# Delta rule layer: the fillers of a stage recorded ahead of the next query and merge, and the transposes of key and value heads 4 to 7 in the scans' Y banks

## The chip, the cores and the metric

One core of a Trainium2 chip runs the whole layer in one launch. The metric is the device time of one execution in microseconds; smaller is better. The engines are TensorE (PE; its weight loads are PEld), VectorE (DVE), ScalarE (ACT), GpSimd (POOL), and SyncE (SP), whose queue issues all DMAs here.

## The reference, cut to what matters

One layer on 1024 tokens of width 1024, with a context of 256 tokens: a token mixer (a Fourier branch and a gated delta rule in both directions, eight heads of 128), merged by gates, then a convolutional FFN. All in fp32. The change lies in the delta rule. For each head, the sequence is first projected and convolved to q, k and v; then per chunk of tokens a triangular system is solved and a state is carried from chunk to chunk:

```
l_mat = where(lower_strict, beta * (k k^T) * decay, 0)
u, w  = triangular_solve(l_mat, [v*beta, k*beta*exp(g)])     # unit diagonal
for each chunk:                                              # the scan
    v_new = u - w @ s
    o     = q_head @ s + (q k^T * decay) @ v_new
    s     = s * exp(g_last) + k_tail^T @ v_new
```

The scan of the context runs first, from a zero state, and gives the states from which the scans of the 1024 tokens start.

## The kernel before, in words

**How it is scheduled.** The program first records all operations, engine by engine and without running them (`Program.record`, L349 is the place where they are all issued later). Then it orders them itself (`schedule`): each operation has a cost in a table, and a rank, which is the longest path of costs behind it to the end of the program, plus a bonus, minus `MIX` = 0.1 of the TensorE cost of all that was recorded before it. Each engine gets its queue in the order in which this planner would start the operations; of those that are ready, the one of the highest rank goes first. The queues are then fixed, and each engine works its queue in order.

**Why the order of recording matters.** A tile is asked for by a tag, and the buffers of a tag are handed out in turn, in the order of recording. The next user of a buffer waits until all uses of the one before it are done. So two things recorded in one order keep it in every buffer that they share, whatever their ranks. PSUM has eight banks, one buffer each: `pp` and `pf` (projections; `pf` for the fillers later), `pd` (score products, query norms), `pm` (the merge), and `X0`, `X1`, `Y0`, `Y1` for the scans of direction 0 and 1. A bank is one buffer, also where only a part of it is used.

**The stages.** `ORDER` names ten stages: c0 and c1 are the context's scans for heads 0 to 3 and 4 to 7; x0 to x7 are the heads on the 1024 tokens, in the order c0, x0, x1, c1, x2 and on to x7. A stage needs, in this order: the projected query and the loaded key (`project_kq`; context stages project nothing there), the decay and score products (`ready_up`, bank `pd`), the inversion of 32x32 blocks on VectorE (`invert`, with a way out to DRAM and back on either side), the merge of those blocks to 128x128 ones by 32- and 64-wide products on TensorE (`merge`, bank `pm`), the loaded keys and values as tokens by channels (`load_kv`), and the scan (`scan_ctx`, `scan_head`). A scan's step of one direction is a chain through TensorE, VectorE and ScalarE: two products in X, then two in Y; with the output there are three. After the last step of a head's scan its outputs are transposed in Y0 and Y1 for a norm (`squares`), and the norm's row, transposed in Y1, is copied out.

**The fillers.** `sides(n)` records the next n projections of a list: k of heads 4 to 7, v of heads 4 to 7, z of eight heads, then gates. Pass 0 of the loop (scan c0) records k4 to k7, pass 1 (scan x0) v4 to v7, each later pass two of the others. `SIDES` has these numbers. A key or value projection (`project_kv`) has 24 matmuls of 256 columns for the context and 48 of 512 columns for the tokens, in three accumulations of which two fit the two banks; its result is convolved into a staging tile `xs`, of which there are two; then ten 128x128 transposes in three groups (`tt`) turn it, ScalarE copies each group out to a tile `tk` (two buffers), and a DMA stores it in DRAM, from where the scans load it. Of keys, ScalarE also squares the group in place. The weights of key, value and query projections go through one ring of three buffers for halves (tags `h`, `l`, each projection takes two of each). The z and gate fillers have weight buffers of their own, which come free when v7 is done.

Of the kernel before, what the change touches and what calls it, by code (L numbers as in the profile page):

```python
# [32 lines left out]
SIDES = (4, 4, 2, 2, 2, 2, 2, 2, 2, 2)  # L33
# [155 lines left out]
class Program:  # L189
# [14 lines left out]
    def close(self, p):  # L204
        self.events.append((False, p))
# [276 lines left out]
def body(tc, a, out):  # L482
    prog = Program(tc)
    layer(prog, a, out)
    prog.run()


def layer(prog, a, out):
# [14 lines left out]
    def ps(tag, shape, name):  # L503
        return psum.tile(shape, F32, tag=tag, name=name, bufs=PPB if tag == "pp" else 1)
# [3 lines left out]
    def bank(shape, name):  # L508
        rota[1] += 1
        return ps(rota[0][rota[1] % len(rota[0])], shape, name)  # L510
# [28 lines left out]
    def weights(src, name, eng=None, tags=("h", "l"), pl=None):  # L539
        return [halves(src[:, o:o + HALF], pl or wst, tags, f"{name}{o}", eng) for o in range(0, src.shape[-1], HALF)]  # L540

    def product(pt, wl, rhs, nk=KT):
        n = 0
        for k in range(nk):
            h, l = rhs(k)
            wh, wlo = wl[k // 4]
            ks = slice((k % 4) * P, (k % 4 + 1) * P)
            for w_, r_ in ((wh, h), (wh, l), (wlo, h)):
                te.matmul(pt, w_[:, ks], r_, start=n == 0, stop=n == 3 * nk - 1)
                n += 1  # L550
# [54 lines left out]
    XY = ("X0", "X1", "Y0", "Y1")  # L605
# [142 lines left out]
    def conv_taps(pt, acc, w3):  # L748
        n = acc.shape[-1]
        se.activation(acc, pt[:, 0:n], AF.Identity, scale=w3[:, 1:2])  # L750
        ve.scalar_tensor_tensor(acc[:, 1:n], pt[:, 0:n - 1], w3[:, 0:1], acc[:, 1:n], op0=ALU.mult, op1=ALU.add)
        ve.scalar_tensor_tensor(acc[:, 0:n - 1], pt[:, 1:n], w3[:, 2:3], acc[:, 0:n - 1], op0=ALU.mult, op1=ALU.add)

    def silu_of_half(acc, name):
        n = acc.shape[-1]
        for o in range(0, n, HALF):
            part = acc[:, o:min(o + HALF, n)]
            th_ = dt("th", f"{name}_{o}", part.shape)
            se.activation(th_, part, AF.Tanh)
            ve.scalar_tensor_tensor(part, th_, 1.0, part, op0=ALU.add, op1=ALU.mult)  # L760
# [79 lines left out]
    def invert_blocks(name, dl):  # L840
        dtt = dram.tile([2 * NU, P, 32], F32, tag="dt", name=f"dt_{name}", bufs=2)
        bl = dt("GR", f"BL_{name}", (P, 32, 32))
        bt = dt("CL", f"BT_{name}", (P, 16, 32))
        btf = bt.rearrange("n c i -> n (c i)")
        po.memset(btf, 0.0)
        for e in range(2):
            es = slice(e * NI, (e + 1) * NI)
            sp.dma_start(bl[es].rearrange("n i j -> n (i j)"), dl.rearrange("u (k i) j -> (u k) (i j)", k=4))
            po.memset(btf[es, e:HALF:34], 1.0)
        lt_ = bl.rearrange("n i j -> n j i")  # L850
        for j in range(31):
            r, w = 31 - j, j // 2 + 1
            tm = dt("tmp", f"tm_{name}{j}", (P, 144))[:, 0:r * w].rearrange("n (w r) -> n w r", r=r)
            ve.tensor_tensor(tm, bt[:, 0:w, j:j + 1].broadcast_to([P, w, r]),
                             lt_[:, j:j + 1, j + 1:32].broadcast_to([P, w, r]), op=ALU.mult)
            ve.tensor_tensor(bt[:, 0:w, j + 1:32], bt[:, 0:w, j + 1:32], tm, op=ALU.subtract)
        for e in range(2):
            sp.dma_start(dtt.rearrange("u (k c e) i -> e (u k) c i", k=4, e=2)[e], bt[e * NI:(e + 1) * NI])
        k2 = dt("CL", f"K2_{name}", (P, 2 * NU, 32))
        sp.dma_start(k2, dtt.rearrange("u p i -> p u i"))  # L860
        return k2
# [80 lines left out]
    def project_kv(w, h):  # L942
        kv = "kv"[w]
        wl = weights((wi_k, wi_v)[w](h), f"{kv}{h}")
        dst = xsp.tile([P, T + TC], F32, tag="xs", name=f"xs{kv}{h}")
        w3 = convw[:, (w + 1) * 8 + h, :]
        pt = bank([P, HALF], f"pc{w}_{h}")
        product(pt[:, 0:TC], wl, hc)
        conv_taps(pt, dst[:, T:T + TC], w3)
        proj_taps(wl, dst, w3, f"x{kv}_{h}")  # L950
        silu_of_half(dst, f"th{kv}{h}")
        if w == 0:
            sp.dma_start(kvd[h], dst)
            ssq = const.tile([P, NCH], F32, tag="ssq", name=f"ssq_k{h}", bufs=3)
        for o in (8, 0, 4):
            n = min(4, NCH - o)
            turn[0] += 1
            tags = XY if h < 4 else ("pm", "pd")
            pt = ps(tags[turn[0] % len(tags)], [P, 4, P], f"tt{kv}{h}_{o}")
            for i in range(n):  # L960
                te.transpose(pt[:, i, :], dst[:, (o + i) * P:(o + i + 1) * P], ident)
            tk = dp.tile([P, 4, P], F32, tag="tk", name=f"tk{kv}{h}_{o}", bufs=2)
            se.activation(tk[:, 0:n, :], pt[:, 0:n, :], AF.Copy)
            sp.dma_start(knd[w, h, :, o:o + n, :], tk[:, 0:n, :])
            if w == 0:
                for i in range(n):
                    se.activation(pt[:, i, :], pt[:, i, :], AF.Square, accum_out=ssq[:, o + i:o + i + 1])
        if w == 0:
            rk = rk_of[:, h, :]
            ve.tensor_scalar(rk, ssq, EPS, None, op0=ALU.add)  # L970
            po.tensor_tensor(rk, rk, mhalf[:, 0:NCH], op=ALU.pow)
# [94 lines left out]
    def proj_taps(wl, dst, w3, name):  # L1066
        edge = const.tile([P, 1], F32, tag="edge", name=f"edge{name}", bufs=2)

        def taps(g, hs, pt):
            conv_taps(pt, dst[:, hs], w3)  # L1070
            if g == 0:
                ve.tensor_copy(edge, pt[:, HALF - 1:HALF])
            else:
                m_ = dst[:, HALF - 1:HALF]
                ve.scalar_tensor_tensor(m_, pt[:, 0:1], w3[:, 2:3], m_, op0=ALU.mult, op1=ALU.add)
                m_ = dst[:, HALF:HALF + 1]
                ve.scalar_tensor_tensor(m_, edge, w3[:, 0:1], m_, op0=ALU.mult, op1=ALU.add)
        proj_rows(wl, hxh, name, taps)
# [86 lines left out]
    @on_stage  # L1165
    def project_kq(i):
        made[i] = stages[i][1](stages[i][5])

    @on_stage
    def load_kv(i):  # L1170
        vals[i] = [stages[i][2](w, stages[i][5]) for w in range(2)]

    @on_stage
    def ready_up(i):
        prep[i] = stages[i][3](stages[i][5], *made[i])

    @on_stage
    def invert(i):
        blocks[i] = invert_blocks(stages[i][0], prep[i][2][2])

    @on_stage
    def merge(i):
        co, _, fl = prep[i]
        merged[i] = merge_blocks(stages[i][0], fl[1], co[2], blocks.pop(i))
# [4 lines left out]
    def sides(n):  # L1189
        for _ in range(min(n, len(rest))):  # L1190
            kind, *which = rest.pop(0)
            if kind == "kv":
                project_kv(*which)
                if which == [1, NH - 1]:
                    close(xsp)
                    close(hcp)
                    enlarge()
            else:
                side(kind, *which)

    def enlarge():
        nonlocal dp2
        rota[0] = ["pp"]
        dp2 = pool("delta2", bufs=1, side="right")
        for t_, n in DB.items():
            if t_ == "fs":
                dp.tags[t_] = [dp2.region(HALF) for _ in range(n)]
            else:
                dp.tags[t_] += [dp2.region(T) for _ in range(n)]
# [6 lines left out]
    for h in range(4):  # L1216
        project_kv(0, h)
# [3 lines left out]
    for h in range(4):  # L1221
        project_kv(1, h)
        if h == 0:
            project_kq(1)
    load_kv(0)
    merge(0)
    for i, (name, _, _, _, scan, n) in enumerate(stages):
        ready_up(i + 1)
        if i:
            load_kv(i)  # L1230
        co, cols, fl = prep.pop(i)
        scan(n, *made.pop(i), *vals.pop(i), co, cols, fl, merged.pop(i))
        invert(i + 1)
        merge(i + 1)
        project_kq(i + 2)
        sides(SIDES[i])
        if i >= 8:
            side("f", 2 * i - 16)
            side("f", 2 * i - 15)
# [558 lines left out]
```

## Time and profile before

| what | value |
|---|---|
| median of 3 runs | 2032.6 us (2032.46 to 2033.29) |
| the profiled execution's own time | 2029.8 us |
| its span in the trace | 2028.1 us |
| mean granted TensorE clock | 0.986 |
| TensorE busy | 1947.3 us, 96% |
| VectorE busy | 1383.4 us, 68% |
| ScalarE busy | 829.1 us, 41% |
| GpSimd busy | 560.0 us, 28% |
| DMA | 257.51 MB, mean 127 GB/s |

The span goes from the first to the last instruction; the profiled execution's own time has 1.7 us around it, and the median of the runs is 2.8 us above that execution. In the trace all instructions stand on one line of code and matmuls carry no names. What a matmul is can be told by its shape (512 or 256 columns: projections; 128: transposes, scores and scans; 64 and 32: merges), and which projection it is by its place, since each engine's records follow the planner's order one for one (an fp32 product counts as two). PEclk is the granted clock, 1.00 for 2.4 GHz and 0.50 for 1.2 GHz, averaged over a stretch.

### The profile page before, as it was taken

How to read it: one execution, taken by the hardware profiler on the slowest of the kernel's cores; microseconds unless marked ns; L12 is line 12 of the kernel's file. 1: busy time of each engine (PE TensorE's matmuls, PEld its weight loads, DVE VectorE, ACT ScalarE, POOL GpSimd, SP SyncE). 2: the span in 40 equal slices, each digit the busy share in tenths (PEclk: the TensorE clock that was granted, in tenths of full speed). 3: DMA queues.
4: the chain of work that ended last, by engine and by line, in shares of the span. 5: the costliest groups of instructions: out<-in, count | busy, mean ns of one | idle time of the engine just before them, and what ended most of it. 6: DMA issues, size and time to landing. Idle time of an engine off the chain costs nothing.

```text
span 2028.1 us, 31373 instructions
## 1 busy us (share of the span) xinstructions
PE 1947.3 (96%) x11470; PEld 1566.6 (77%) x11470; DVE 1383.4 (68%) x2868; ACT 829.1 (41%) x1948; POOL 560.0 (28%) x573
## 2 busy tenths in 40 slices
PE   7989999799999999999999999979999999999998
PEld 3878878687787788878787778757788888778886
DVE  5649767767777688673756484579989889873132
ACT  5565345454345454533431132454344444632121
POOL 3120111101111110210321000358778888500000
PEclk9999999899999999999999999999999999999999
DMA  7153333344434453431778562312222222543231
GB/s 301 53 194 96 98 118 105 113 141 136 123 93 114 139 154 101 122 115 51 233 250 288 181 233 80 114 53 72 102 73 83 84 78 89 179 169 104 73 125 52
DMA packets 180636, 257.51 MB, mean 127 GB/s; under 512 B 75921, under 2 KB 97522, under 8 KB 180482
## 3 DMA queue, kind: packets, MB, share of 16 engines
q1 hardware_dynamic: 180482, 255.51, 39.3%
q8 instruction: 90, 1.47, 0.3%
q14 instruction: 64, 0.52, 0.1%
HBM read 194.52 MB, written 60.94 MB: 126 GB/s over the span
## 4 chain that ended last, share of the span: by engine, by line
PE 75%; DVE 11%; DMA 5%; ACT 4%; issue 2%; POOL 1%; SPq 0%; DVEq 0%; POOLq 0%; ACTq 0%
PE p L349 75%; DVE m L349 9%; ACT m L349 3%; DVE p L349 3%; DMA d<-m 2%; DMA m<-d 2%; POOL m L349 1%; ACT p L349 0%; SPq L349 0%; DMA m<-in_wu_dram 0%; ACT L349 0%; DVEq L1787 0%; POOLq L1787 0%; ACTq L349 0%; DVEq L349 0%
## 5 line engine op out<-in xcount | busy, mean ns | idle before, releaser
L349 PE MATMUL p<-m,m 128*128 128x512 f32 (+5 forms) x11310 | 1933.7, 337 | 72.9 <-ACT m L349 28.1
L349 PEld LDWEIGHTS p<-m,m 128*128 128x128 f32 (+3 forms) x11310 | 1548.6, 173 | 449.5 <-ACT m L349 64.6
L349 DVE TENSOR_TENSOR m<-m,m 128x512 fp32r<-128x512 f32 (+22 forms) x1116 | 579.6, 535 | 236.3 <-ACT m L349 207.7
L349 ACT ACTIVATE m<-m 128x512 fp32r<-128x512 f32 (+8 forms) x669 | 431.7, 663 | 636.0 <-DMA m<-d 165.5
L349 POOL TENSOR_TENSOR m<-m,m 128x512 fp32r<-128x512 f32 (+5 forms) x338 | 450.9, 1357 | 817.2 <-DVE m L349 660.9
L349 ACT ACTIVATE m<-p 128x512 f32<-128x512 f32 (+5 forms) x510 | 220.3, 447 | 324.1 <-PE p L349 289.0
L349 DVE SCALAR_TENSOR_TENSOR m<-p,m,m 128x128 f32<-128x128 f32 (+4 forms) x488 | 203.4, 451 | 105.5 <-ACT m L349 56.6
L349 DVE SCALAR_TENSOR_TENSOR p<-m,m,p 128x512 f32<-128x512 f32 x352 | 240.2, 750 | 2.7 <-ACT p L349 0.4
L349 ACT ACTIVATE m<-p,m 128x128 f32<-128x128 f32 (+2 forms) x240 | 115.5, 494 | 184.0 <-PE p L349 182.5
L349 POOL MEMSET m<- 128x1024 f32 (+7 forms) x79 | 35.7, 459 | 370.7 <-PE p L349 220.9
L349 POOL COPY m<-m 32x256 f32<-32x256 f32 (+2 forms) x136 | 54.6, 404 | 202.8 <-DMA m<-d 156.6
L349 DVE COPY m<-p 32x256 f32<-32x256 f32 (+11 forms) x116 | 42.0, 367 | 53.1 <-PE p L349 26.8
L349 DVE TENSOR_TENSOR m<-p,m 128x512 f32<-128x512 f32 (+4 forms) x91 | 57.8, 644 | 28.4 <-PE p L349 25.3
L349 DVE SCALAR_TENSOR_TENSOR m<-m,m 128x512 f32<-128x512 f32 (+5 forms) x119 | 66.0, 558 | 16.4 <-ACT m L349 9.1
L349 DVE SCALAR_TENSOR_TENSOR m<-m,m,m 128x1024 f32<-128x1024 f32 (+2 forms) x68 | 57.8, 854 | 17.0 <-DMA m<-in_w_ada_dram 16.7
L349 DVE TENSOR_TENSOR m<-m,p 128x128 f32<-128x128 f32 (+3 forms) x117 | 53.6, 459 | 23.1 <-PE p L349 22.4
L349 ACT ACTIVATE p<-p 128x128 f32<-128x128 f32 x208 | 55.2, 265 | 23.1 <-PE p L349 21.4
L349 DVE SCALAR_TENSOR_TENSOR m<-m,p 128x512 f32<-128x512 f32 x76 | 50.7, 683 | 17.8 <-ACT m L349 7.8
L349 DVE SCALAR_TENSOR_TENSOR m<-m,m,p 128x128 f32<-128x128 f32 x128 | 42.8, 341 | 25.9 <-PE p L349 25.1
L349 DVE SCALAR_TENSOR_TENSOR m<-m 128x1 f32<-128x1 f32 (+1 forms) x25 | 5.4, 216 | 52.9 <-ACT m L349 52.8
L349 ACT ACTIVATION_READ_ACCUMULATOR p<-p 128x1 f32 x208 | 39.5, 190 | 0.0
L349 ACT ACTIVATE p<-m,m 128x512 f32<-128x512 f32 x44 | 30.3, 691 | 21.6 <-DVE m L349 21.2
(20 smaller groups left out, 160.3 us busy)
## 6 DMA issues: line engine op xcount, KB each, us to landing
m<-d SPq DMA_DIRECT2D x76, 512.0 KB
d<-m SPq DMA_DIRECT2D x138, 256.0 KB
m<-d SPq DMA_DIRECT2D x114, 256.0 KB
m<-in_wi_dram SPq DMA_DIRECT2D x106, 256.0 KB
m<-in_w_ada_dram SPq DMA_DIRECT2D x48, 512.0 KB
m<-in_wu_dram SPq DMA_DIRECT2D x88, 256.0 KB
m<-in_wn_dram SPq DMA_DIRECT2D x26, 512.0 KB
m<-d SPq DMA_DIRECT2D x44, 192.0 KB
```

The source lines that it names most:

```text
L349: return getattr(engine.real, method)(*[real(v) for v in args], **{k_: real(v) for k_, v in kw.items()})
```

## The change

Two edits. In `project_kv`, the transposes of heads 4 to 7 alternate between the banks Y0 and Y1 instead of `pm` and `pd`; heads 0 to 3 keep the four banks X0, X1, Y0 and Y1. In the loop over the stages, the fillers of pass i are recorded ahead of the query projection of stage i + 2, and this ahead of the merge of stage i + 1; before, it was merge, query, fillers. What is computed doesn't change, nor does any instruction's shape.

```diff
@@ project_kv
         for o in (8, 0, 4):
             n = min(4, NCH - o)
             turn[0] += 1
-            tags = XY if h < 4 else ("pm", "pd")
+            tags = XY if h < 4 else ("Y0", "Y1")
             pt = ps(tags[turn[0] % len(tags)], [P, 4, P], f"tt{kv}{h}_{o}")
@@ layer, loop over the stages
         scan(n, *made.pop(i), *vals.pop(i), co, cols, fl, merged.pop(i))
         invert(i + 1)
+        sides(SIDES[i])
+        project_kq(i + 2)
         merge(i + 1)
-        project_kq(i + 2)
-        sides(SIDES[i])
         if i >= 8:
```

## Rows read from the trace of the kernel before

**Rows 1.** The page, part 1: engine, busy us, share of the span, instructions.
```profile
PE 1947.3 (96%) x11470; PEld 1566.6 (77%) x11470; DVE 1383.4 (68%) x2868; ACT 829.1 (41%) x1948; POOL 560.0 (28%) x573
```

**Rows 2.** Waits of TensorE over the whole span: total us, times, longest.
```profile
PE p L349 <- ACT m L349: 28.1, 28, 2.6
PE p L349 <- DVE m L349: 23.6, 34, 3.7
```

**Rows 3.** Windows by stage: length, busy us (instructions) of each engine, PEclk, DMA.
```profile
280.00:303.00 23.00, 19.17 (x292) 15.44 (x291) 11.71 (x29) 8.27 (x28) 8.82 (x17) 0.93 0.36 116
...
381.00:403.00 22.00, 12.60 (x248) 10.24 (x249) 13.07 (x21) 12.37 (x32) 7.70 (x17) 0.72 0.56 194
...
461.00:480.00 19.00, 16.69 (x77) 12.74 (x76) 18.47 (x51) 14.58 (x45) 2.31 (x2) 0.91 0.59 217
480.00:920.00 440.00, 430.45 (x3797) 352.86 (x3796) 322.00 (x945) 191.39 (x569) 77.36 (x143) 1.00 0.40 116
```

**Rows 4.** Timeline of TensorE, 378 to 426: start, length, count, [idle before].
```profile
381.21 2.08 PE L349 MATMUL p<-m,m 128*128 128x128 f32 x72 [0.38 <-DVE m L349]
...
390.64 1.97 PE L349 MATMUL p<-m,m 64*64 64x64 f32 x32 [2.34 <-DVE m L349]
393.59 4.31 PE L349 MATMUL p<-m,m 64*64 64x64 f32 x41 [0.98 <-ACT m L349]
399.70 0.44 PE L349 MATMUL p<-m,m 128*128 128x128 f32 x2 [1.80 <-ACT m L349]
400.94 9.47 PE L349 MATMUL p<-m,m 128*128 128x512 f32 x42 [0.80 <-DVE m L349]
```

**Rows 5.** Timeline of TensorE from 213 to 322, some lines.
```profile
232.97 17.27 PE L349 MATMUL p<-m,m 128*128 128x256 f32 x99 [0.42 <-DVE m L349]
...
278.69 4.73 PE L349 MATMUL p<-m,m 128*128 128x128 f32 x146 [0.33 <-ACT m L349]
...
293.05 0.65 PE L349 MATMUL p<-m,m 128*128 128x128 f32 x4 [0.39 <-DVE m L349]
295.56 31.67 PE L349 MATMUL p<-m,m 128*128 128x512 f32 x166 [1.86 <-ACT p L349]
...
319.21 2.87 PE L349 MATMUL p<-m,m 128*128 128x256 f32 x22
```

**Rows 6.** Timeline of ScalarE around the ends and starts of scans.
```profile
327.50 0.27 ACT L349 ACTIVATE m<-p 128x128 f32<-128x128 f32 x1
...
382.56 0.26 ACT L349 ACTIVATE p<-p 128x128 f32<-128x128 f32 x1 [2.27 <-PE p L349]
...
397.05 0.25 ACT L349 ACTIVATE m<-p 8x128 f32<-8x128 f32 x1
...
425.10 0.29 ACT L349 ACTIVATE m<-p 128x128 f32<-128x128 f32 x1
...
445.96 0.60 ACT L349 ACTIVATE m<-p 128x512 f32<-128x512 f32 x1 [0.27 <-PE p L349]
```

**Rows 7.** Timeline of GpSimd, 378 to 404: the power of the norm of x0.
```profile
387.00 1.62 POOL L349 TENSOR_TENSOR m<-m,m 128x8 f32<-128x8 f32 x1
```

**Rows 8.** The chain of waits in order of time: its longest piece, in the FFN.
```profile
1470.52 282.92 PE p L349 x1235
```

**Rows 9.** Waits of the SP queue, 376 to 432 us.
```profile
SPq L349 <- ACT m L349: 20.8, 7, 11.7
```

**Rows 10.** Windows of the scans of c0 and c1, columns as in rows 3.
```profile
249.50:292.70 43.20, 40.38 (x430) 33.43 (x428) 30.77 (x94) 21.35 (x72) 9.52 (x19) 1.00 0.32 95
506.80:531.50 24.70, 24.37 (x150) 20.18 (x149) 21.89 (x74) 11.96 (x40) 4.66 (x6) 1.00 0.37 92
```

## The prediction

> **What bounds the kernel now.** Read the engines' totals first: TensorE is busy for 1947.3 of 2028.1 us, the next engine (VectorE) for 68% [rows 1]. So the kernel is bound by TensorE, and a change that neither removes nor adds a matmul, as this one, can only move TensorE's 81 us of idle time and its half-clock time. Then the totals of TensorE's waits: 28.1 us ended by ScalarE, 23.6 us by VectorE, in pieces of at most 3.7 us [rows 2]; no single large wait is to be had. Third, the windows by stage [rows 3], where the reader should see three weak stretches in the part that the diff touches. A stretch loses its idle time and, in half clock, busy time times (1 - PEclk):
> - A, 280 to 303 us: 23.0 - 19.17 = 3.8 idle, and 19.17 x 0.07 = 1.3 of clock, 5.1 us.
> - B, 381 to 403 us: 22.0 - 12.60 = 9.4, and 12.60 x 0.28 = 3.5, 12.9 us; a granted clock of 0.72 is a mean of the 1.2 and 2.4 GHz levels.
> - C, 461 to 480 us: 2.3 and 1.5, 3.8 us.
> From 480 to 920 us, where the z and gate fillers run, the idle share is 9.55 of 440 us, 2%. The whole prize is 21.8 us, 1.1%.
>
> The timeline tells what B is [rows 4]. The scan of x0 has ended and its norm is transposed at 381.21; then come only 32x32 and 64x64 products, the merge of x1, with gaps of 1.0 to 2.3 us between its steps; the last transposes of v4 and v5 come up to 400.14, and the first wide matmul, the second half of v6's projection, at 400.94. v6 waited because its staging tile is v4's, one of v4's transposes was recorded behind the merge in the bank pm, and so could run only when the merge was over. A is the same on the key side [rows 5]: the stretch of products of 128 columns and less from 278.69 on is the scan of c0 and the merge of x0, one group of k4's transposes follows at 293.05, and the second half of k6's projection starts at 295.56.
>
> **The change part by part.** Price of a projection: 1235 wide matmuls (512 columns) took 282.92 us in a dense stretch [rows 8], 0.229 us each. A query or filler projection has 48 of them, 11.0 us. A key or value has 24 of 256 columns besides, at half the price by estimate: 2.7 more, 13.7 us.
>
> (1) The transposes' banks. No instruction is added: per head still 10 transposes in three groups, two banks. In the old order of the bank pm: merge x0, k4 to k7, merge x1, v4 to v7, merge c1; pd has the score products and the query norms between. In the new one Y0 and Y1: scan c0, k4 to k7, scan x0, its norm, v4 to v7, scan x1. So v4's transposes wait for the end of scan x0 instead of the end of merge x1. Y0 is free when its four squares are done, which begin at 382.56: at 384 by estimate; Y1 only when the transposed norm is copied out, which was at 397.05 [rows 6] but hangs on the power on GpSimd that ended at 388.6 [rows 7]; with two short steps more, 389.5. From v4's last transposes, the end of the row at 393.59, to v6's matmul it took 3.0 us before (397.90 to 400.94) [rows 4]. So v6's second half may start between 388 (both needed groups early) and 393.5, 7 to 13 us sooner than at 400.94. Work for the hole is there: 24 wide matmuls of v6, 5.5 us, and v7's 13.7, together 19.2 us beside a merge that TensorE serves in short bursts. I take 10 us off B, its bounds being 0 (nothing starts sooner) and 12.9 (all of it). What is late next is the weights: SP waited 20.8 us for ScalarE's results in 376 to 432 us [rows 9], since its queue is in order and the writes of transposed tiles stand ahead of v7's weights; these writes come earlier now too.
>
> What queues behind the new wait: on TensorE the transposes stand in order among the projections, on ScalarE their copies, on SP their stores. Scan x0 now waits for k7's transposes and scan x1 for v7's. I price both at nothing: in the old trace the first plain copy of a product of scan x0 came only at 327.50, behind k7's projection (v4's first matmuls, at 319.21, follow it [rows 5]), and that of scan x1 at 425.10, 29 us after the merge, while v7's last transposes were copied at 445.96 [rows 6]. If v7 comes 10 us sooner, its transposes are out at about 436, so scan x1 starts up to 11 us later than it did. Meanwhile TensorE has the z projections and a query, 11.0 us each, which no scan holds back. Bounds: 0, and +11 us where none of these has its weights in time; I take the 0.
>
> (2) The query after the fillers. It matters once, in pass 0: weights go through a ring of three buffers in recorded order, so the query projection of x1 (11.0 us, which stood ahead of k4's first matmuls at 232.97 [rows 5]) now follows k7. k4 and k5 move up by as much, but k6's second half needs k4's staging tile, and k4's transposes now need the end of scan c0, at about 292.7. Between k6's first half and that end, no projection is to be had. Bounds: if scan c0 ends when it did, 11.0 us of query work falls behind 295.56 that stood ahead of it: +11.0. If scan c0 moves to the front, it can do with the 24.7 us that the same scan of c1 took, as against 43.2 [rows 10]; it started at 249.5, so it ends at about 274, and the 18.5 us saved outweigh the 11.0: -5.1, for no more than A's loss can be won. The planner ranks an operation by the longest path behind it; k6, k7, the query and scan x0 now all hang on scan c0's last product, so its rank rises above k5's projection. I take 0, between the ends and nearer the front case.
>
> (3) The merge after the fillers, and all later passes. The z, g and f fillers have buffers and a bank (pf) of their own, so only ranks move: MIX is 0.1 of the TensorE time recorded ahead, two fillers are 22.0 us, so the merge loses 2.2 us of rank and a little for the query, the fillers gain about as much as one query and merge. The ranks compared are paths of hundreds of us. The stretch to 920 has 2% idle; a different interleaving is worth -3 to +3 us, and I take 0. C hangs on values of c1 and on ScalarE; 0, bounds 0 and -3.8.
>
> Sum: -10 + 0 + 0 + 0 = -10 on the profiled execution's 2029.8 us, 2019.8. The median of the runs is 2032.6, 2.8 us above that execution, so 2022.6 in its terms.
>
> The Trainium skill, "PSUM — Partial Sum Buffer", section "Engine vs sequencer instructions", says that matmuls start and complete in program order. The trace agrees: at 293.05 and 295.56 all wide matmuls of TensorE stand behind four transposes. By that rule every transpose placed too early behind a scan would stop the fillers too; what that does to the time is the slower rival below, worked out from rows alone.
>
> **The rivals.**
> - Slower: the scan becomes the gate. Scan c0 isn't run at the front, k4's transposes wait until about 292, and the query of x1, lost as filler, is done after it: +11.0 us. At the same time B stays, because Y1 is held until 397 by the norm. 2032.6 + 11.0 = 2043.6. For it: scan c0 took 43.2 us beside the projections. Against: scan c1's 24.7. The point from which it decides: k6's second half, at 295.56 before, must come 11.0 us sooner for the query to be paid for; from 284.6 on each us later is a us lost.
> - Nothing: the hole changes its place. The transposes wait for the norm as long as they did for the merge, and stage 0 comes out even: 2032.6. For it: the norm's copy at 397.05 is as late as the merge's end [rows 6]. Against: it was late because ScalarE did other work from 385 to 397, the norm's power having ended at 388.6.
> - More: A, B and C all close, since the scans move up too: 2032.6 - 21.8 = 2010.8. Against: VectorE has 68% of its own.
> - That the change does nothing at all can't be: the bank tags of 16 projections change.
>
> **How the numbers follow.** Forecast (2014 to 2028) 0.42; more 0.15; nothing 0.18; slower 0.25. Within 0.2% is 4 us, about what a measurement of this kernel can tell from no change. Faster is 0.42 + 0.15 = 0.57, same 0.18, slower 0.25. The range goes from 2006 (the full prize and 5 us of interleaving) to 2044 (the slower rival); its own bounds summed are -12.9 - 5.1 - 3 - 3.8 = -24.8 and 0 + 11.0 + 11.0 + 3 = +25.0, and the ends of these are left out.
>
> **What would show it.** Right: in the new trace the stretch of scan x0's end and merge x1 has wide matmuls between the merge's small ones, its idle time is under 3 us and its clock above 0.9. Wrong: wide matmuls stop for more than 10 us while scan c0 or scan x0 ends (slower rival), or the first wide matmul after scan x0 still follows merge x1 (nothing). The query step is judged by when k7 and the query of x1 are both done: before 319.21; at about 319 by my zero, at 330 by the slower rival.

## The result, and the profile after

The changed kernel took 2008.93 us (median of 4 runs, 2007.74 to 2010.38), the kernel before 2032.53 us beside it: ratio 0.9887, 95% interval 0.9869 to 0.9904, so 23.6 us less. The forecast was 10 us less. Sign and range held; the size was that of the rival "More" (2010.8), which had a chance of 0.15.

TensorE did the same work in the same busy time. Part 1 of the page of the changed kernel (its span is 2006.0 us), against [rows 1]:

```profile
PE 1947.3 (97%) x11470; PEld 1562.6 (78%) x11470; DVE 1388.3 (69%) x2868; ACT 829.7 (41%) x1948; POOL 565.0 (28%) x573
```

1947.3 us of both spans are busy, so by this count the 22.1 us of span came out of TensorE's idle time: 80.8 us before, 58.7 us now. The mean granted clock is 0.991, beside 0.986 before. TensorE's waits over the whole span, in us, times and longest, against [rows 2]:

```profile
PE p L349 <- DVE m L349: 17.9, 29, 3.7
PE p L349 <- ACT m L349: 17.0, 17, 2.6
```

5.7 us less on VectorE and 11.1 us less on ScalarE. Where the time went is read from windows of the same stages, which now lie elsewhere in time. The changed kernel, columns as in [rows 3] (length, busy us of PE, PEld, DVE, ACT and POOL, PEclk, DMA):

```profile
254.00:290.00 36.00, 35.35 (x195) 29.94 (x194) 33.01 (x99) 19.93 (x66) 4.02 (x2) 1.00 0.52 164
...
353.00:408.00 55.00, 53.93 (x465) 42.25 (x464) 41.74 (x98) 25.17 (x57) 10.84 (x20) 1.00 0.55 159
...
447.00:466.00 19.00, 16.48 (x255) 12.41 (x255) 10.48 (x19) 15.00 (x48) 9.19 (x17) 1.00 0.70 235
466.00:900.00 434.00, 427.31 (x3641) 353.97 (x3640) 325.20 (x945) 192.93 (x576) 72.52 (x128) 1.00 0.40 117
```

From the end of scan c0 to the end of k7 (A's place) 0.65 us are idle; from the end of scan x0 to the end of v7, with the norm and merge x1 in it (B's place), 1.07 us; both at a granted clock of 1.00. C's place, behind scan x1, still idles 2.5 us (2.3 before), now without half clock. Beside merge x1 the wide matmuls now run, as a grouping of TensorE's instructions by shape shows for 376 to 400 us (count, busy us, mean ns, idle before):

```profile
L349 PE MATMUL p<-m,m 128*128 128x512 f32 x35 | 10.4, 413 | 0.0
L349 PE MATMUL p<-m,m 128*128 128x256 f32 x24 | 6.0, 330 | 0.0
L349 PE MATMUL p<-m,m 64*64 64x64 f32 x64 | 5.8, 237 | 0.0
...
L349 PE MATMUL p<-m,m 32*32 32x32 f32 x158 | 2.4, 194 | 0.0
```

The 32- and 64-column rows are the merge, the two first rows v6 and v7; in [rows 4] the same merge stood alone, with idle times of 1.0 to 2.3 us. From 200 to 480 us the widest pauses between the starts of two matmuls of the projections were 26.5 us (from 374.4, in B) and 20.0 us (from 275.6, in A and ahead of it); now the widest is 4.6 us (from 312.0). Lines of ScalarE's timeline that answer to [rows 6], in the same order:

```profile
320.96 0.27 ACT L349 ACTIVATE m<-p 128x128 f32<-128x128 f32 x1
...
354.36 0.26 ACT L349 ACTIVATE p<-p 128x128 f32<-128x128 f32 x1 [2.54 <-PE p L349]
...
361.47 0.25 ACT L349 ACTIVATE m<-p 8x128 f32<-8x128 f32 x1
...
415.32 0.28 ACT L349 ACTIVATE m<-p 128x128 f32<-128x128 f32 x1
...
419.29 0.59 ACT L349 ACTIVATE m<-p 128x512 f32<-128x512 f32 x1
```

The norm is copied out 7.1 us after its first square (14.5 before). The first copy of a product of scan x0 comes 6.5 us sooner, that of scan x1 9.8 us, v7's last 26.7 us.

### The profile page after: what moved, and what is told of

It is laid out like the page before. It is cut to its first block, busy times and chain, and to the rows that moved or that the text cites. A ratio compares the mean times of both kernels' runs of the same rounds, so it can differ in the third digit from the quotient of the medians.

```text
span 2006.0 us, 31360 instructions
## 1 busy us (share of the span) xinstructions
PE 1947.3 (97%) x11470; PEld 1562.6 (78%) x11470; DVE 1388.3 (69%) x2868; ACT 829.7 (41%) x1948; POOL 565.0 (28%) x573
## 4 chain that ended last, share of the span: by engine, by line
PE 74%; DVE 11%; DMA 5%; ACT 4%; issue 2%; POOL 1%; SPq 0%; DVEq 0%; POOLq 0%; ACTq 0%
PE p L349 74%; DVE m L349 10%; ACT m L349 4%; DMA m<-d 2%; DMA d<-m 2%; DVE p L349 2%; POOL m L349 1%; DMA m<-in_wi_dram 1%; ACT p L349 1%; DMA m<-in_wu_dram 0%; DMA m<-in_w_ada_dram 0%; SPq L349 0%; ACT L349 0%; DVEq L1787 0%; POOLq L1787 0%
## 5 line engine op out<-in xcount | busy, mean ns | idle before, releaser
L349 PE MATMUL p<-m,m 128*128 128x512 f32 (+5 forms) x11310 | 1934.3, 336 | 49.1 <-DVE m L349 17.9
L349 PEld LDWEIGHTS p<-m,m 128*128 128x128 f32 (+3 forms) x11310 | 1544.4, 172 | 429.7 <-issue 53.7
L349 DVE TENSOR_TENSOR m<-m,m 128x512 fp32r<-128x512 f32 (+27 forms) x1116 | 584.1, 539 | 242.6 <-ACT m L349 215.6
L349 ACT ACTIVATE m<-p 128x512 f32<-128x512 f32 (+4 forms) x510 | 220.9, 447 | 306.9 <-PE p L349 270.2
L349 POOL COPY m<-m 32x256 f32<-32x256 f32 (+2 forms) x136 | 60.6, 448 | 149.6 <-DMA m<-d 112.2
L349 DVE SCALAR_TENSOR_TENSOR m<-m,m 128x512 f32<-128x512 f32 (+5 forms) x119 | 66.0, 560 | 24.7 <-ACT m L349 19.5
L349 DVE SCALAR_TENSOR_TENSOR m<-m,m,p 128x128 f32<-128x128 f32 x128 | 43.3, 341 | 23.2 <-PE p L349 22.5
L349 ACT ACTIVATE p<-m,m 128x512 f32<-128x512 f32 x44 | 30.2, 691 | 21.6 <-DVE m L349 21.3
```

The costliest lines, as they stand in the source:

```text
L349: return getattr(engine.real, method)(*[real(v) for v in args], **{k_: real(v) for k_, v in kw.items()})
```

## The experiments

Each was timed in rounds against the kernel before on the same chip; intervals are 95%. The letters in the expectations name theories that are spelled out there. Two readings of all runs come first, since single experiments are read from them.

**Landmarks** (ends, in us, of what TensorE does for each; "turned" is the last of its transposes; told by place, since the records follow the planner's order):

| kernel | query of x1 | k7 turned | scan c0 | scan x0 | v7 turned | scan x1 | scan x4 | scan x7 |
|---|---|---|---|---|---|---|---|---|
| before | 230.6 | 329.2 | 292.7 | 380.8 | 444.1 | 460.9 | 738.0 | 959.2 |
| changed | 301.1 | 316.8 | 254.0 | 352.8 | 417.5 | 446.5 | 705.2 | 933.8 |
| e1_banks | 231.0 | 330.4 | 274.3 | 363.4 | 426.5 | 455.9 | 719.8 | 960.0 |
| e2_order | 300.7 | 308.6 | 342.3 | 407.4 | 420.5 | 468.4 | 730.7 | 953.9 |
| e3_query | 230.3 | 326.6 | 271.2 | 363.7 | 430.2 | 461.9 | 722.9 | 959.2 |
| e12_front | 232.0 | 329.8 | 253.4 | 365.5 | 434.3 | 465.7 | 725.7 | 963.8 |
| e8_front | 229.4 | 329.3 | 264.2 | 379.9 | 446.6 | 462.9 | 741.2 | 962.9 |
| e11_split | 273.7 | 326.2 | 271.8 | 361.7 | 429.7 | 461.1 | 719.4 | 949.7 |

**Lost time.** In a stretch each matmul that TensorE starts is counted at its price in dense stretches (0.229 us for 512 columns, 0.115 for 256, 0.110 for 128, 0.029 for 64, 0.016 for 32); what lacks to the stretch's length is lost: in idle time, at half clock, or in matmuls that are shown longer than at their price. It is an estimate; between two kernels the difference counts. One profiled execution each, in us:

| banks, query of x1 | kernel | 100–250 | 250–400 | 400–600 | 600–700 | 700–900 | 0–1000 |
|---|---|---|---|---|---|---|---|
| old, ahead | before | 15.4 | 28.6 | 23.2 | 14.8 | 14.1 | 134.4 |
| old, ahead | mean of 4 | 14.2 | 30.2 | 23.9 | 15.2 | 15.7 | 137.5 |
| new, ahead | e1_banks | 20.8 | 16.1 | 27.2 | 11.1 | 22.7 | 136.0 |
| new, ahead | mean of 4 | 19.0 | 22.6 | 27.4 | 11.8 | 20.6 | 140.0 |
| old, behind | mean of 2 | 15.8 | 21.0 | 21.8 | 20.7 | 16.0 | 132.7 |
| new, behind | changed | 11.9 | 18.7 | 20.5 | 8.2 | 14.2 | 109.2 |
| new, behind | mean of 5 | 14.2 | 17.9 | 22.8 | 7.8 | 17.0 | 116.2 |

These counts see more than idle time does. In B's place (353 to 408) the changed kernel idles 1.07 us and loses 8.8 by the count; B itself (381 to 403) lost 14.3.

The means are of before, m_b11, e8_front and e5_late; e1_banks, e3_query, e12_front and m_e111; e2_order and m_e211; the changed kernel, e4_merge, m_a11, m_a09 and e5_early (whose passes 2 to 9 keep the old order). The profiled executions of e1_banks and m_e111 were 6.8 and 14.1 us above their medians, so the row of the new banks with the query ahead is too high by some us.

**Each edit alone.**

```diff
e1_banks (from before)
-            tags = XY if h < 4 else ("pm", "pd")
+            tags = XY if h < 4 else ("Y0", "Y1")
e2_order (from before)
-        merge(i + 1)
-        project_kq(i + 2)
         sides(SIDES[i])
+        project_kq(i + 2)
+        merge(i + 1)
```

Expected of e1_banks: 

> The bank edit alone; the old order of recording (merge, query, fillers) stays. Theory R (rank: the transposes of k4 to v7 now hang on the scans' ends, so the scans and all that leads to them rise in the planner's rank; the fillers' order is secondary): 2008 to 2014 us, scan of c0 over before 265 us. Theory W (waits: the gain is that the transposes no longer stand behind a merge in pm): also 2008 to 2014, but the scan of c0 needn't be early. Theory Q (query: the gain comes from k4 to k7 being ahead of the query of x1): 2028 to 2034, since the query keeps its place.

Expected of e2_order: 

> The order of recording alone (fillers, query, merge); the transposes stay in pm and pd, where they now stand ahead of the next merge instead of behind it. R: the scans are not tied to the transposes, 2026 to 2034 us. W: no transpose stands behind a merge here either, 2010 to 2020. Q: the query is late as in the changed kernel, 2008 to 2015.

Measured: e1_banks 2030.43 us, 0.9997 [0.9981, 1.0012]; e2_order 2024.18 us, 0.9959 [0.9943, 0.9974]. The sum of the two is -0.44%, the change gave -1.13%: they pay together. e1_banks falls in Q's range alone, e2_order in none of the three. Windows of e1_banks, columns as above:

```profile
200.00:250.00 50.00, 47.09 (x424) 37.02 (x423) 32.97 (x88) 17.82 (x42) 7.34 (x17) 0.97 0.34 89
250.00:400.00 150.00, 147.54 (x1249) 122.51 (x1248) 110.91 (x317) 77.14 (x251) 30.07 (x46) 1.00 0.39 118
...
700.00:900.00 200.00, 191.18 (x1634) 159.22 (x1635) 146.04 (x423) 85.21 (x259) 35.45 (x59) 0.98 0.41 119
```

The same two last windows of the kernel before:

```profile
250.00:400.00 150.00, 135.15 (x1185) 115.18 (x1183) 106.45 (x296) 76.31 (x249) 29.26 (x46) 0.95 0.37 111
...
700.00:900.00 200.00, 197.82 (x1694) 164.94 (x1694) 156.09 (x458) 92.16 (x281) 35.62 (x61) 1.00 0.42 123
```

So with the banks alone B closes (12.4 us of idle time go from 250 to 400, the clock rises from 0.95 to 1.00) and scan x4 ends 18 us sooner; then it is given back, idle time of 8.8 us against 2.2 from 700 to 900, and scan x7 ends no sooner. 5.4 us more were lost at 100 to 250. In e2_order nothing ties scan c0 to the key transposes any more; it is spread over 268 to 342 us, and all of scan x0 follows late. B closes here too, though the transposes are in `pm` and `pd`: they stand ahead of the merge now, and merge x1 waits for them and begins at 419.1 instead of 381.8. So e2_order is no test of the query alone. Its windows:

```profile
250.00:300.00 50.00, 48.31 (x272) 41.07 (x271) 41.70 (x124) 27.47 (x93) 8.19 (x12) 1.00 0.45 130
300.00:350.00 50.00, 49.84 (x417) 36.56 (x416) 22.98 (x60) 21.88 (x77) 9.07 (x14) 0.90 0.27 80
350.00:400.00 50.00, 49.70 (x312) 43.55 (x310) 42.67 (x131) 20.43 (x56) 3.01 (x5) 1.00 0.37 103
```

The second of these looks 99.7% busy and loses 16.1 us by the count. Its clock is 0.90, and a merge's matmuls are shown far longer in it than elsewhere. TensorE by shape in this stretch:

```profile
L349 PE MATMUL p<-m,m 64*64 64x64 f32 x64 | 6.4, 239 | 0.0
L349 PE MATMUL p<-m,m 32*32 32x32 f32 x160 | 5.3, 216 | 0.0
```

As many of both in the kernel before, 480 to 530 us, in a dense stretch:

```profile
L349 PE MATMUL p<-m,m 64*64 64x64 f32 x64 | 2.6, 222 | 0.0
L349 PE MATMUL p<-m,m 32*32 32x32 f32 x160 | 2.4, 194 | 0.0
```

The mean of one (ns) hardly differs, the time that they fill (us) is more than double: they stand in short groups between wide matmuls (512 columns) and 128-column ones. Such a change of shape has a price in these traces. In the kernel before, from 200 to 960 us, the median time from the start of a wide matmul to the next start is 231 ns where that is a wide one too (1368 times), and 320 ns where it is a product of a merge (51 times); behind a product of a merge it is 121 ns to a wide one (50 times) and 7 ns to another of its kind (2180 times). With 128 columns in place of 512 it is alike: 205 ns to a merge's product, 112 ns to another of 128. One excursion to the merge thus costs some 0.2 us by estimate. In e2_order 22 of them lie between 320 and 340 us, at clocks of 0.98 and 1.00: 4.4 of the 8.1 us lost there. Another 5.6 us are lost in the ten ahead, at the lower level of the clock:

```profile
310.00:320.00 10.00, 10.00 (x84) 6.32 (x84) 1.99 (x5) 2.62 (x10) 2.14 (x2) 0.51 0.10 38
```

The changed kernel has 21 such excursions in B's place, 4.2 of the 8.8 us lost there.

**Query or merge, and which passes.**

```diff
e3_query (from the changed kernel)
-        sides(SIDES[i])
         project_kq(i + 2)
+        sides(SIDES[i])
         merge(i + 1)
e4_merge (from the changed kernel)
+        merge(i + 1)
         sides(SIDES[i])
         project_kq(i + 2)
-        merge(i + 1)
e5_early (changed kernel: new order in passes 0 and 1 alone)
+        if i < 2:
...
e5_late (old banks: new order in passes 2 to 9 alone)
+        if i >= 2:
...
```

Expected of e3_query: 

> The new banks, and in the loop the query, then the fillers, then the merge: against the changed kernel the query of x1 alone goes back ahead of k4 to k7. Theory I (interaction: the banks close A and B, but only with k4 and k5 recorded ahead of the query is there enough to do while the scan of c0 runs alone at 210 to 250 us, where the bank edit alone lost 8 us): 2018 to 2030 us, with the loss at 200 to 250 us. Theory J (jitter: the planner answers every shift of ranks with some us, and the changed kernel is a lucky draw of many): anywhere from 2008 to 2030, with the loss spread over the passes.

Expected of e4_merge: 

> The new banks, and in the loop the merge, then the fillers, then the query: against the changed kernel the merge alone goes back. The merge shares no buffer with fillers or query, so only its rank moves, by some 3 us. I: as the changed kernel, 2005 to 2013 us. J: 2005 to 2025, a difference of 5 us or more from so small a shift being nothing special.

Expected of e5_early: 

> Both edits, but the new order in passes 0 and 1 only; passes 2 to 9 record merge, query, fillers as before. If the gain is made in the stages with key and value fillers (R, W and Q alike): 2006 to 2013 us. If the later passes' order carries part of it: 2013 to 2025.

Expected of e5_late: 

> The new order in passes 2 to 9 only, old banks; nothing of the key and value fillers changes, only ranks of later fillers, queries and merges. R, W and Q: 2029 to 2036 us, no change. If the later passes matter: 2015 to 2028.

Measured: e3_query 2040.84 us, 1.0034 [1.0022, 1.0047]; e4_merge 2014.24 us, 0.9892 [0.9876, 0.9908]; e5_early 2023.47 us, 0.9962 [0.9944, 0.9979]; e5_late 2032.29 us, 0.9999 [0.9988, 1.0011]. With the new banks the merge's place is worth nothing, and the query's 1.4% (e3_query against e4_merge). e3_query is slower than both of its theories allowed, and it moves the queries of all passes, not that of x1 alone as its expectation has it; e4_merge fell out of I's range and into J's.

Which passes matter is read from e5_early, the step between e1_banks and the changed kernel. It has all landmarks of the changed kernel to 2 or 3 us as far as scan x4 (707.2), but scan x7 ends at 947.3, not 933.8:

| from | to | what changes | end of scan x4 | end of scan x7 | time |
|---|---|---|---|---|---|
| e1_banks | e5_early | the order in passes 0 and 1 | 12.6 us sooner | 12.7 us sooner | 7.1 us less |
| e5_early | changed | the order in passes 2 to 9 | 2.0 us sooner | 13.5 us sooner | 15.2 us less |

So with the new banks the later passes' order goes with the larger part of the gain, as the second theory of e5_early had it (2013 to 2025). With the old banks it gains nothing (e5_late). The count from 700 to 900 us says the same of all runs with Y0 and Y1: 19 to 23 us are lost in the five whose passes 2 to 9 record the query ahead of the fillers (e1_banks, e3_query, e12_front, m_e111, e5_early), 13 to 18 in the five that record it behind (changed, e4_merge, m_a11, m_a09, e11_split). With the old banks there is no such gap: 14 to 15 us ahead (before, m_b11, e8_front), 15 to 19 behind (e2_order, m_e211, e5_late). In these passes query and fillers share no buffer, so only ranks differ, and chance of the order isn't excluded; which wait the later order spares was not traced.

**How much is chance of the order.** `MIX` weighs the order of recording in all ranks; another value gives another interleaving of the same work in the same buffers.

```diff
-MIX = 0.1
+MIX = 0.11
```

m_a11 and m_a09 are the changed kernel with 0.11 and 0.09, m_b11 the kernel before, m_e111 e1_banks and m_e211 e2_order with 0.11.

Expected of m_a11: 

> The changed kernel with MIX = 0.11 instead of 0.1: every rank moves a little, no buffer's order does. I: 2005 to 2013 us, since the order of the buffers makes the gain. J: 2010 to 2025, as other draws are worse than the one that was kept.

Expected of m_b11: 

> The kernel before with MIX = 0.11. I: 2029 to 2036 us. J: 2018 to 2045, since a shift of ranks moves this one by several us as well.

Expected of m_a09: 

> The changed kernel with MIX = 0.09. If its time is a lucky draw of the planner: 2014 to 2026 us. If the order of the buffers makes the gain and the planner scatters by some 6 us: 2003 to 2018.

Expected of m_e111: 

> The new banks with the old order (merge, query, fillers) and MIX = 0.11: a second draw of the bank edit alone, which made no difference. If the banks alone are worth nothing: 2026 to 2040 us. If the first draw was an unlucky one: 2010 to 2024.

Expected of m_e211: 

> The old banks with the new order (fillers, query, merge) and MIX = 0.11: a second draw of the order alone, which gained 8 us. If the order alone is worth 8 us: 2018 to 2030. If that was scatter: 2028 to 2042.

| | MIX 0.10 | MIX 0.11 | MIX 0.09 |
|---|---|---|---|
| neither edit | 1 | 1.0029 [1.0018, 1.0040] | |
| banks alone | 0.9997 [0.9981, 1.0012] | 1.0000 [0.9975, 1.0025] | |
| order alone | 0.9959 [0.9943, 0.9974] | 0.9979 [0.9963, 0.9995] | |
| both | 0.9887 [0.9869, 0.9904] | 0.9922 [0.9907, 0.9937] | 0.9922 [0.9903, 0.9940] |

Another MIX alone moves a kernel by 0.03 to 0.35%, up to 7 us. m_a11 and m_b11 lie outside I's ranges and in J's: the planner scatters by more than I allowed. The gain of both edits holds: 0.9922/1.0029 = 0.9893 at 0.11. That it exceeds the sum of the two single gains holds in size only in part: by 0.69% at 0.10, by 0.28% at 0.11 (1.0000 + 0.9979 - 1.0029 = 0.9950 against 0.9922).

**Is it scan c0's early end?** In the changed kernel scan c0 runs at the front and ends at 254.0. Two kernels force it there by a bonus of 60,000 on its ranks, with the query left ahead: with the old banks, and with the new ones.

```diff
e8_front (from before); e12_front (from e3_query) has the same lines
+        prog.bonus = 6e4 if i == 0 else 0.0
         scan(n, *made.pop(i), *vals.pop(i), co, cols, fl, merged.pop(i))
+        prog.bonus = 0.0
e12_front also
+        prog.bonus = 6e4 if h > 1 else 0.0
         project_kv(1, h)
+        prog.bonus = 0.0
...
+    prog.bonus = 6e4
     load_kv(0)
     merge(0)
+    prog.bonus = 0.0
```

Expected of e8_front: 

> The kernel before, with 60,000 added to the rank of each operation of the scan of c0, and nothing else: the scan goes to the front of every queue, while the transposes stay in pm and pd behind the merges. If the early scan of c0 is what makes the gain: 2012 to 2024 us. If it is the transposes no longer standing behind the merges, with the scan as their gate: 2028 to 2036, k4's last transposes still behind merge x0 at about 290 and hole B as before.

Expected of e12_front: 

> The new banks with the order query, fillers, merge, and 60,000 added to the rank of the projections of v2 and v3, the loads and the merge of c0 and its scan: the query of x1 stays ahead of k4 to k7 in the weights' ring and the projections' banks, but its work no longer stands ahead of what leads to the scan of c0. Theory V (the query costs because its work on VectorE and ScalarE delays the scan of c0): scan c0 starts at 224 to 230 us, 2012 to 2024 us in all. Theory Q2 (it costs by its place in the ring: the query is spent before the scan and k4 comes late): scan c0 early as well, but 2030 to 2042 us.

Measured: e8_front 2036.39 us, 1.0024 [1.0013, 1.0035]; e12_front 2041.93 us, 1.0045 [1.0029, 1.0062]. In both scan c0 ended early (264.2 and 253.4), and nothing was won. In e8_front B stays, as a window shows (the kernel before has 40.34 us busy there, at a clock of 0.90):

```profile
350.00:400.00 50.00, 38.71 (x442) 33.94 (x440) 36.10 (x103) 22.88 (x66) 12.13 (x20) 0.86 0.39 112
```

In e12_front the bank is free as early as in the changed kernel, and yet k7 is turned at 329.8 instead of 316.8, v7 at 434.3 instead of 417.5, and scan x1 ends 19.2 us later. So what the query holds up in pass 0 is the row of projections behind it, also where the scan ends early. The time of 2041.93 us is in Q2's range; that this row alone makes it isn't shown, since e12_front also has the queries ahead in all later passes.

**The query halfway.**

```diff
e11_split (from the changed kernel)
-        sides(SIDES[i])
+        sides(2 if i == 0 else SIDES[i])
         project_kq(i + 2)
+        sides(2 if i == 0 else 0)
```

Expected of e11_split: 

> The changed kernel, but in pass 0 the query of x1 stands between k5 and k6 instead of behind k7. Theory V (VectorE: what counts is that the query's convolution and scores don't stand ahead of the last multiplications that the scan of c0 needs; behind k5 it is late enough, and it then fills the wait of k6 for the scan): 2000 to 2012 us, scan of c0 starting before 232. Theory K (the key projections must come first, since scan x0 waits for k7's transposes): 2014 to 2024, scan x0 later by the query's 11 us.

Measured: 2021.15 us, 0.9958 [0.9944, 0.9972]. With the query of x1 between k5 and k6 the time lies between that of the query ahead (e3_query, 1.0034) and behind (0.9887); k7 is turned at 326.2, beside 326.6 and 316.8. Only pass 0 differs from the changed kernel here, so the query's place in this pass goes with 14.4 us (0.9887 to 0.9958); time and scan x0, 8.9 us later, fit theory K and not V. But the row's lateness doesn't set the time by itself: e3_query has k7, scan c0, scan x0, v7 and scan x1 within 2 us of e11_split, and is 15.4 us slower. Besides the query's exact place in pass 0, these two differ in the order of the later passes, whose price above is of this size.

**Which banks.**

```diff
e6_xbanks (from the changed kernel)
+            tags = XY if h < 4 else ("X0", "X1")
e7_four (from the changed kernel)
+            tags = XY
```

Expected of e6_xbanks: 

> The changed kernel with the transposes of heads 4 to 7 in X0 and X1 instead of Y0 and Y1. The norm after a scan doesn't use these, so v4's transposes needn't wait for its end. If the norm's hold on Y1 costs something: 1998 to 2005 us, v4's transposes 5 us or more sooner than at 361.8. If not: 2005 to 2016, the same within the planner's scatter of some 6 us.

Expected of e7_four: 

> The changed kernel with the transposes of heads 4 to 7 in all four of X0, X1, Y0 and Y1, as heads 0 to 3 have them. If two banks hold the transposes up (each is held by four transposes, a copy and, of keys, four squares): 1998 to 2006 us. If the waits are for the scan and the staging tiles: 2006 to 2016.

Measured: e6_xbanks 2024.50 us, 0.9963 [0.9950, 0.9977]; e7_four 2022.60 us, 0.9954 [0.9939, 0.9969]. Both are slower than their theories allowed. X is free of the norm, but v4's transposes come only 0.6 us sooner (361.2), and scan x0 ends at 367.6 instead of 352.8. Four banks gain less than two: in e7_four k7 is turned 8.9 us sooner than in the changed kernel, v7 9.1 us later. The Trainium skill, "Perfetto Trace Analysis", section "Matmul Optimizations", advises to make use of all eight PSUM banks; here all eight are in use in every kernel, and the one that gives the transposes two more of them gained less (0.9954 against 0.9887). A likely reason, not shown, is that each bank brings the order of its other users with it.

## Why the prediction was right or wrong

- **What bounds it, and B's mechanism: right.** TensorE's busy time did not move, and wide matmuls run beside merge x1; idle time there is 1.07 us and the clock 1.00, where the text asked for under 3 us and above 0.9. That B hung on transposes recorded behind the merge in `pm` is shown from several sides: it closes with the bank edit alone, closes as well where they keep `pm` but are recorded ahead of the merge (e2_order), and stays with scan c0 early alone.
- **Step (1), "I take 10 us off B": right for the stretch, wrong as a term of a sum.** Alone it took 12.5 us off the lost time from 250 to 400, but 0.6 us off the whole (5.9 at MIX 0.11; ratios are taken times 2032.5 us here): the rest was given back elsewhere. On top of the new order it was worth 14.6 us (0.9959 to 0.9887), or 11.6 at 0.11. The waits that it brings, priced at nothing, cost nothing that the landmarks show: the first copies of scans x0 and x1 come 6.5 and 9.8 us sooner.
- **Step (2), "I take 0, between the ends and nearer the front case": this is the step that failed.** On top of the new banks the new order gained 22.4 us (0.9997 to 0.9887; 15.9 at MIX 0.11), with a merge whose place is worth nothing there; the bounds were -5.1 to +11.0. Its pass 0, of which step (2) speaks, is worth 7.1 us with pass 1 (e1_banks to e5_early) and 14.4 us where the query goes only half the way back (e11_split, one ordering each). Scan c0 did move to the front, and took 29.7 us there (224.3 to 254.0), nearer the 24.7 assumed than the 43.2 of before. The error is the bound "no more than A's loss can be won" and the sentence behind it, that k7 and the query would both be done at about 319: they were done at 301.1. I treated the query as filler that changes places with k4 to k7 and asked only what hole A pays. But k4 to k7 and v4 to v7 follow each other through one ring and two staging tiles, and what stands ahead of them delays them all: with the query behind, k7 is turned 13.0 us sooner than in e12_front and v7 16.8 us, though scan c0 ended together in both. The query itself has no such row behind it: its norm and the score products of x1 follow from 304 to 372 us, and merge x1, which needs them, begins at 374.5, beside 381.8 before. That the query delays the row is shown; how much of the whole this delay makes is not settled by those two prices, since MIX alone moves a kernel by up to 7 us.
- **Step (3), 0 for the merge: right with the new banks** (0.9892 against 0.9887). **0 for all later passes, within -3 to +3: not borne out.** With the new banks their order goes with 15.2 us (e5_early to the changed kernel), with the old ones with none (e5_late). MIX alone moves a kernel by up to 7 us, so part of the 15.2 may be chance; the cause is open.
- **The sum.** Three holes were priced one by one, 21.8 us in all. What the changed kernel gained lies partly elsewhere: of its 25.2 us less lost, 9.9 lie in 250 to 400, 2.7 in 400 to 600, 6.6 in 600 to 700, 3.5 in 100 to 250. These 3.5 were all won before 200 us, ahead of all that the edits move (k4's first matmul is at 206.5), so a change of ranks made them, or chance of the one execution. Behind 1000 us some 3 us were given back, as the span is 22.1 us shorter. The prize left out what is lost while TensorE is shown busy. "More" came in its time and only in part as told: A and B closed by idle time and clock, but 250 to 400 as a whole won 9.9 us and not their 18.0, and C kept its idle time. That the total is the size of the three holes is luck.
- **Slower and nothing.** The slower rival's mechanism is not seen in the changed kernel, since scan c0 is at the front. With the new banks, slower came only with the query ahead (e3_query and e12_front, 7 and 9 us), and in e12_front not by the scan, which ended at 253.4.

Open: how much of the gain is chance of the interleaving. The same banks and place of the query gave 0.9887 and 0.9892, and at another MIX 0.9922 twice, where scan x7 ends at 939.7 and 944.3 instead of 933.8. Why the order of the later passes matters only with the new banks was not traced to a wait.

## What to carry to other kernels

When work is recorded or issued in order through a small ring, ask of each piece how long a row stands behind it, not which hole it fills: a piece that is needed late belongs behind a row that is needed early (here 7 to 14 us by two comparisons). Price edits that share buffers together, since a hole closed alone can open again 300 us later; the end of the last common stage tells more than the hole. Before the last half per cent is explained, draw the schedule anew with a constant changed a little, for both kernels.

## What the runs showed that was not expected

- A busy TensorE can lose more than an idle one: 16.1 us in a stretch shown 99.7% busy (e2_order, 300 to 350), against 11.6 us in one of the kernel before that is shown 90% busy (250 to 300, 44.97 of 50).
- One program's executions can differ more than two programs do: m_e111 took 2016.8 to 2046.9 us in 12 runs and e1_banks 2023.3 to 2039.0, the kernel before 2027.4 to 2038.8 and 2025.6 to 2038.2 beside them, in 26 and 24. The scatter goes with the mean granted clock: m_e111's fastest run had 0.991 and its slowest 0.977, e1_banks' 0.992 and 0.984. Why the clock differs from run to run wasn't found; the intervals above hold it.
- From 100 to 200 us, ahead of all edits, the changed kernel idles 4.3 us and the kernel before 7.2, and the clock is 1.00 instead of 0.97. The changed kernel first, then the kernel before:

```profile
100.00:200.00 100.00, 95.66 (x510) 79.79 (x509) 75.92 (x193) 63.87 (x175) 11.01 (x18) 1.00 0.45 149
```

```profile
100.00:200.00 100.00, 92.82 (x490) 77.97 (x489) 72.03 (x184) 60.89 (x176) 11.73 (x18) 0.97 0.45 142
```
